# A two-layer recurrent trunk on eight cores: four token groups, two in flight under one schedule, in place of three groups in turn

## The chip, the cores and the metric

One Trainium2 chip, all eight cores; each core runs the same program on its own tokens. The time is that of the slowest core in device microseconds, median of several runs. A program on all eight cores has a second, slower state, in which the cores of one die (0 to 3 or 4 to 7), sometimes both, show a lower granted clock; comparisons here use fast runs alone. PE is TensorE, PEld its weight loads, DVE VectorE, ACT ScalarE, POOL GpSimd, SP SyncE. The granted clock is the share of PE's full clock that the profile shows. PSUM banks are the eight buffers that the matmuls of this program write to.

## The reference, cut to what matters

```python
def trunk(x, ...):                       # layer 0: even mixer (GLA and HGRN2 heads); layer 1: odd mixer (retention)
    for l in range(2):
        nw = norm_w[l]
        x = x + 0.5 * rmsnorm(swiglu(rmsnorm(x, nw[0]), gate[l, 0], up[l, 0], down[l, 0]), nw[1])
        m = mixer(rmsnorm(x, nw[2]), state, ...)      # chunked recurrence, carries a state along the sequence
        x = x + rmsnorm(m, nw[3])
        x = x + 0.5 * rmsnorm(swiglu(rmsnorm(x, nw[4]), gate[l, 1], up[l, 1], down[l, 1]), nw[5])

def swiglu(x, w_gate, w_up, w_down):
    return (silu(x @ w_gate) * (x @ w_up)) @ w_down   # 1024 -> 2816 -> 1024
```

A core has one prompt sequence of 2048 tokens and 16 samples of 8 tokens with states of their own: 2176 tokens, 1024 channels. A group of tokens goes through six stages in order: feed-forward network (FFN), even mixer, FFN, FFN, odd mixer, FFN. Every stage starts with a norm of the residual `x` (pre-norm) and ends with a norm of its own output that is added to `x` (post-norm). So between two stages of one group nothing but norm work can be done. Two groups depend on each other only through the mixers' states.

## The kernel before: the parts concerned

Three groups of 768, 768 and 640 tokens, in turn. Every operation is recorded with its dependences and an estimated cost; a list scheduler then reorders each engine's instructions within a window of 512, and fences (`S.barrier`) stand around the mixers:

```python
for g, tiles in enumerate(GROUP_TILES):                 # 3 groups
    dma_sp(X[:, :, 0:nt], xv[:, :, col0:col0 + nt], ...)
    for l in range(2):
        prenorm(l, 0, nt); ffn(l, 0, nt); postnorm_residual(l, 1, nt, True)
        prenorm(l, 2, nt)
        S.barrier()
        mixer_even(g, tiles, nt) if l == 0 else mixer_odd(g, tiles, nt)
        S.barrier()
        out_proj(...); postnorm_residual(l, 3, nt, False)
        prenorm(l, 4, nt); ffn(l, 1, nt); postnorm_residual(l, 5, nt, True, ...)
# PSUM banks are named for a purpose
PSA, PSB, PSC, PSN = PS[0:2], PS[2:4], PS[4:6], PS[6]
```

The FFN's gate, the statistics of a norm (squares, a matmul with a matrix of ones, logarithm and exponential) and a mask in the mixer, which goes head by head:

```python
act(SGT[..], pg, AF.Silu, ...)                          # one ScalarE function, with a table of its own
tt(HB[:, jj, ..], SGT[..], pu, ALU.mult, ...)
...
for kc in range(nch): act(XN[:, kc, ..], src(kc), AF.Square, ...)     # rms_stats
for kc in range(nch): mm(PSN, ONES, XN[:, kc, ..], ...)
act(LNT, PSN, AF.Ln, ...); act(RS, LNT, AF.Exp, ..., scale=-0.5)
...
for h in range(4):
    tt(PT[..][:, h*128+64:h*128+128], psc[:, h*128+64:h*128+128], MASK0[..], ALU.mult, ...)
```

## Time and profile before

| | before |
|---|---|
| median of the first 4 runs | 4512.52 us (4509.89 to 4714.66) |
| matmuls / DVE / ACT instructions | 21,738 / 3656 / 3002 |
| PE busy, mean granted clock of the profiled core | 75%, 0.84 |
| DMA share of the two data queues | 39.7% + 8.1% |

The prediction below shows the slices and the stages. Two more views of the profile before are used later. First the busy line and the chain that ended last (shares of the span by engine); PE is 61% of that chain, so nearly 40% of the time the end hung on something else:

```profile
PE 3395.3 (75%) x21738; PEld 2074.6 (46%) x21738; DVE 1727.7 (38%) x3656; ACT 1470.8 (33%) x3002; POOL 336.1 (7%) x640
...
PE 61%; DVE 17%; DMA 7%; issue 7%; ACT 6%; SPq 1%; DVEq 1%; ACTq 0%; POOLq 0%
```

Then PE's waits (who waited, for whom, total us, times, longest). `XN` holds the squares and the normalised input: 341.8 us are waits of the statistics for ScalarE's squares, at the borders of stages. Three of them (43.8, 44.6 and 42.2 us) stand at the start and at the two changes of group, where the squares themselves waited for the load of the tokens. `S0B` is one of the mixers' own tiles:

```profile
PE PS L528 <- ACT XN L541: 341.8, 232, 44.6
PE PS L528 <- ACT S0B L541: 130.5, 48, 8.0
...
```

### The profile page before, as it was taken

The page shows a single profiled execution, that of the slowest core. Times are in us where ns is not written, and L with a number is a line of the kernel's source. Part 1 is how long each engine was busy: PE and PEld are TensorE (multiplying, and loading weights), DVE is VectorE, ACT ScalarE, POOL GpSimd, SP SyncE. Part 2 cuts the span into 40 slices and gives each one's busy share as a digit, 9 for nine tenths or more (in the row PEclk, how much of TensorE's full clock was granted, in tenths as well). Part 3 has the DMA queues.
Part 4 walks back from the last instruction along what each step waited for, and adds up shares of the span by engine and source line. Part 5 has one row for each costly group of instructions (what it writes and reads, how often), then busy time and mean ns, then how long its engine had stood idle before and what let it go on. Part 6 is the DMA issues. An engine that isn't in the chain of part 4 may idle for free.

```text
span 4504.0 us, 65698 instructions; the slowest of 8 cores (4488.4 to 4504.0 us)
## 1 busy us (share of the span) xinstructions
PE 3395.3 (75%) x21738; PEld 2074.6 (46%) x21738; DVE 1727.7 (38%) x3656; ACT 1470.8 (33%) x3002; POOL 336.1 (7%) x640
## 2 busy tenths in 40 slices
PE   5956698978796977489888779596536987664487
PEld 3633364645453544345445546373224665431255
DVE  2144514157423143531335641314453234455433
ACT  1235322234421223532224432224343223332232
POOL 1100010100010000001000001010000110000010
PEclk9977799989798987689999879797657998875598
DMA  6622264634355542246453336473224755676554
GB/s 121 94 40 44 46 101 75 102 61 76 60 87 111 92 67 43 41 71 104 75 90 72 77 56 103 103 116 53 61 68 99 121 93 87 148 207 194 172 90 84
DMA packets 172824, 405.79 MB, mean 90 GB/s; under 512 B 18112, under 2 KB 46672, under 8 KB 172496
## 3 DMA queue, kind: packets, MB, share of 16 engines
q0 software_dynamic: 91472, 286.47, 39.7%
q1 hardware_dynamic: 81024, 115.11, 8.1%
q8 instruction: 185, 3.03, 0.3%
q14 instruction: 143, 1.17, 0.1%
HBM read 632.51 MB, written 55.44 MB: 153 GB/s over the span
## 4 chain that ended last, share of the span: by engine, by line
PE 61%; DVE 17%; DMA 7%; issue 7%; ACT 6%; SPq 1%; DVEq 1%; ACTq 0%; POOLq 0%
PE PS L528 60%; DVE TMP L557 5%; ACT YB L541 3%; DVE X L545 3%; DMA ret_s<-S0F 2%; DVE YB L545 2%; DMA S0F<-sret 2%; DMA X<-xT 2%; DVE S0F L557 1%; DVE PT L545 1%; DVE XN L557 1%; ACT L541 1%; SPq L521 1%; DVEq L296 1%; ACT XN L541 1%
## 5 line engine op out<-in xcount | busy, mean ns | idle before, releaser
L528 PE MATMUL PS<-XN,WS 128*128 128x384 bf16 (+1 forms) x10992 | 1820.8, 327 | 172.3 <-ACT YB L541 59.2
L528 PEld LDWEIGHTS PS<-XN,WS 128*128 128x128 bf16 x10992 | 1090.9, 100 | 861.6 <-issue 290.9
L528 PE MATMUL PS<-HB,WD 128*128 128x384 bf16 (+1 forms) x5376 | 845.5, 320 | 24.8 <-DVE HB L545 24.8
L545 DVE TENSOR_TENSOR HB<-SGT,PS 128x384 bf16<-128x384 f32 (+1 forms) x528 | 280.7, 532 | 1296.5 <-PE PS L528 1292.4
L528 PEld LDWEIGHTS PS<-HB,WD 128*128 128x128 bf16 x5376 | 529.8, 99 | 336.1 <-issue 41.4
L541 ACT ACTIVATE SGT<-PS 128x384 f32<-128x384 f32 (+1 forms) x528 | 250.0, 473 | 993.4 <-PE PS L528 989.9
L528 PE MATMUL PS<-XN,ONES 128*128 128x384 bf16 (+1 forms) x576 | 175.4, 387 | 382.7 <-ACT XN L541 341.8
L541 ACT ACTIVATE YB<-PS 128x384 f32<-128x384 f32 (+2 forms) x432 | 204.0, 472 | 457.7 <-PE PS L528 430.2
L528 PEld LDWEIGHTS PS<-XN,ONES 128*128 128x128 bf16 x576 | 57.8, 103 | 493.4 <-issue 479.3
L525 POOL DMA_DIRECT2D WS<-wgu x264 | 139.4, 528 | 1682.4 <-PE PS L528 1634.6
L541 ACT ACTIVATE XN<-YB 128x384 bf16<-128x384 f32 (+1 forms) x288 | 145.5, 505 | 257.9 <-DVE YB L545 236.2
L528 PE MATMUL PS<-WS,XN 128*128 128x256 bf16 x1632 | 210.5, 283 | 24.3 <-DMA WS<-ewin 22.6
L541 ACT ACTIVATE XN<-X 128x384 bf16<-128x384 f32 (+1 forms) x288 | 140.4, 502 | 259.4 <-DVE X L545 160.8
L545 DVE TENSOR_TENSOR YB<-PS,YB 128x384 f32<-128x384 f32 (+1 forms) x204 | 109.2, 535 | 239.8 <-PE PS L528 239.8
L528 PEld LDWEIGHTS PS<-WS,XN 128*128 128x128 bf16 x1632 | 162.5, 102 | 57.2 <-issue 30.5
L557 DVE SCALAR_TENSOR_TENSOR XN<-X,NW,RS 128x384 bf16<-128x384 f32 (+1 forms) x288 | 147.5, 588 | 81.9 <-PE PS L528 49.6
L541 ACT ACTIVATE S0B<-S0F 128x1024 bf16<-128x1024 f32 (+2 forms) x96 | 83.6, 877 | 266.5 <-DMA S0F<-sret 181.4
L528 PE MATMUL PS<-VX,KDT 128*128 128x512 bf16 (+2 forms) x224 | 87.5, 451 | 98.6 <-DVE S0F L557 89.7
L557 DVE SCALAR_TENSOR_TENSOR S0F<-S0F,PS 128x512 f32<-128x512 f32 x128 | 87.8, 686 | 181.3 <-ACT S0B L541 122.2
L528 PE MATMUL PS<-YB 128*128 128x64 bf16 (+2 forms) x408 | 70.3, 240 | 99.2 <-ACT YB L541 36.3
L525 POOL DMA_DIRECT2D WD<-wd x192 | 101.4, 529 | 565.8 <-PE PS L528 549.0
L557 DVE SCALAR_TENSOR_TENSOR TMP<-YB,NW,RS 128x384 f32<-128x384 f32 (+1 forms) x96 | 57.1, 595 | 220.7 <-PE PS L528 211.9
(105 smaller groups left out, 2511.1 us busy)
## 6 DMA issues: line engine op xcount, KB each, us to landing
WS<-wgu POOLq DMA_DIRECT2D x264, 512.0 KB, 6.0
WD<-wd POOLq DMA_DIRECT2D x192, 352.0 KB, 5.0
WS<-owin POOLq DMA_DIRECT2D x72, 512.0 KB, 6.3
S0F<-sret SPq DMA_DIRECT2D x64, 512.0 KB, 4.7
ret_s<-S0F SPq DMA_DIRECT2D x128, 256.0 KB, 3.9
WS<-ewin POOLq DMA_DIRECT2D x30, 512.0 KB, 5.5
WD<-owout POOLq DMA_DIRECT2D x24, 512.0 KB, 6.2
X<-xT SPq DMA_DIRECT2D x2, 3072.0 KB, 29.7
```

Source lines behind the costliest of these rows:

```text
L296: eng.wait_ge(self.esem[src], val)
L521: return S.dma("sp", lambda e, o=out, i=in_: e.dma_start(out=o, in_=i), key, reads, writes, nbytes=nb)
L525: return S.dma("pool", lambda e, o=out, i=in_: e.dma_start(out=o, in_=i), key, reads, writes, nbytes=nb)
L528: return S.op("pe", lambda e, o=out, l=lhsT, r=rhs, a=start, b=stop: e.matmul(o, l, r, start=a, stop=b), reads, writes, cost=max(fsz(rhs), ...
L541: return S.op("act", lambda e, o=out, i=in_, f=func, k=kw: e.activation(out=o, in_=i, func=f, **k), reads, writes, cost=fsz(out) / 1400.0 ...
L545: return S.op(eng, lambda e, o=out, a=in0, b=in1, p=op: e.tensor_tensor(out=o, in0=a, in1=b, op=p), reads, writes, cost=fsz(out) / 960.0 + ...
L557: return S.op("dve", lambda e, o=out, a=in0, x=sc, b=in1, p=op0, q=op1: e.scalar_tensor_tensor(out=o, in0=a, scalar=x, in1=b, op0=p, op1=q ...
```

## The change

The intent is to keep PE busy through mixers and norms with the FFN of another group. The diff rewrites most of the program (1227 added lines, 1125 removed); its core, with cuts:

```diff
-GROUP_TILES = [[0, 1, 2, 3, 4, 5], [6, 7, 8, 9, 10, 11], [12, 13, 14, 15, 16]]
-NTM = 768
-WINDOW = 512
+NG = 4                                  # groups of 544 tokens: 512 of the prompt and 4 samples
+BN = [256, 288]                         # column blocks of one group
...
+class Sched:                            # one list scheduler over all engines and the whole program
+    CAP = {"F": 6, "M": 5}              # PSUM banks that the FFN chain and the mixer chain may hold, of 8
+    MFRAC = 0.85
...
-for g, tiles in enumerate(GROUP_TILES): ...            # FFN, fence, mixer, fence, FFN
+    F(0, 0, 0)                          # F(slot, group, which): stages of one slot run side by side
+    for pr in range(2):
+        a, b = 2 * pr, 2 * pr + 1
+        ...
+        M(sl, a, 0); F(sl, b, 0); sl += 1
+        F(sl, a, 1); M(sl, b, 0); F(sl, a, 2); sl += 1
+        F(sl, b, 1); M(sl, a, 1); F(sl, b, 2); sl += 1
+        F(sl, a, 3); M(sl, b, 1); ...
...
-act(SGT[bi % 2][:, 0:bn], pg[:, 0:bn], AF.Silu, ...)
+act(e, PV(pg[b], 0, BN[b]), AF.Exp, [], re_, scale=-1.0)
+act(e, e, AF.Ln, re_, re_, bias=1.0)
+act(e, e, AF.Exp, re_, re_, scale=-1.0)
+tt(e, PV(pg[b], 0, BN[b]), e, ALU.mult, re_, re_)
...
-for h in range(4):
-    tt(PT[pk][:, h * 128 + 64:h * 128 + 128], psc[...], MASK0[:, kind, 64:128], ALU.mult, ...)
+tt(pv[:, :, 64:128], PV(psc, ...), MASK[:, 64:128].unsqueeze(1).to_broadcast([128, 4, 64]), ALU.mult, ...)
...
+    pend.append((m, b))                 # statistics of a block's post-norm run while the next block is projected
+    if len(pend) > 2: stats_mm(pns[b_], b_, m_, Yv(s, m_, b_), RY(s, m_, b_))
```

A PSUM tile gets whichever bank is free when the scheduler places it. Weights are read four times instead of three.

## The prediction

> **What bounds the kernel now.** I read the cores' spans first: 4488 to 4504 us at a granted clock of 0.841 to 0.846, both dies alike, so a fast run (one of the four timed runs, 4714.66 us, is slow; I predict the fast state). Then the 40 slices of the page:
>
> ```profile
> ## 2 busy tenths in 40 slices
> PE   5956698978796977489888779596536987664487
> ...
> PEclk9977799989798987689999879797657998875598
> DMA  6622264634355542246453336473224755676554
> ```
>
> PE swings between 9 and 4, the clock swings with it, and no other engine is full where PE is not. So this is not one bound but stages in turn. The table of windows, cut at stage borders that I found from the long matmul runs of the timeline, tells them apart (columns: stretch, length, busy us of PE, PEld, DVE, ACT and POOL with instruction counts, granted clock, DMA share, GB/s):
>
> ```profile
> 0.00:53.00 53.00, 6.00 (x17) 2.18 (x18) 4.20 (x14) 9.11 (x20) 6.14 (x15) 1.00 0.78 156
> ...
> 227.00:533.00 306.00, 178.39 (x1025) 103.15 (x1024) 150.00 (x357) 142.60 (x318) 14.68 (x28) 0.72 0.25 40
> 533.00:707.00 174.00, 173.62 (x1059) 103.68 (x1057) 39.85 (x73) 39.60 (x78) 19.53 (x37) 0.99 0.59 97
> 707.00:734.00 27.00, 9.60 (x32) 2.98 (x31) 20.24 (x35) 12.89 (x24) 0.53 (x1) 0.68 0.13 23
> ...
> 908.00:1250.00 342.00, 258.14 (x1730) 156.53 (x1729) 199.84 (x412) 146.26 (x272) 17.42 (x33) 0.85 0.34 62
> ...
> 3453.00:3597.00 144.00, 143.48 (x1052) 103.03 (x1051) 32.01 (x67) 34.91 (x77) 19.86 (x38) 1.00 0.73 117
> ...
> 3768.00:4325.00 557.00, 312.29 (x2186) 179.33 (x2184) 267.09 (x546) 190.97 (x316) 17.26 (x33) 0.68 0.58 157
> ...
> 4471.00:4504.00 33.00, 3.06 (x19) 1.62 (x16) 17.00 (x33) 3.83 (x7) 0.00 (x0) 0.56 0.21 80
> ```
>
> 533:707 is one feed-forward (FFN) of 768 tokens: PE full, DVE and ACT under a quarter. 227:533 is the even mixer with its norms, 908:1250 the odd mixer, 3768:4325 the odd mixer of the last group with all sample states: PE 56 to 75% and part of that at a low clock, DVE and ACT about half, each waiting for another. 707:734 is norm work between two FFNs. There are twelve FFN stretches, 8 of 174 us and 4 of 144 (640 tokens): 1968 us. The other 2536 us hold little PE work. How little needs the price of a matmul:
>
> ```profile
> 140.33 57.36 PE L528 MATMUL PS<-XN,WS 128*128 128x384 bf16 x352
> ...
> 311.70 7.15 PE L528 MATMUL PS<-WS,XN 128*128 128x256 bf16 x64
> ```
>
> 57.36/352 = 163 ns for 384 columns. 7.15 us for 64, less about 0.2 us for the last one's drain, is 109 ns for 256. Both fit columns/2.4 + 2 ns. In a dense stretch 128-column matmuls start about 55 ns apart, which I take as the least price. Over all 21,738 matmuls of this kernel (6.98 million columns) that is 2992 us at full clock. So PE has 2992 us to do in 4504, and 1512 us are idle or lost to the low clock.
>
> **What the Trainium skill says.** "Perfetto Trace Analysis", section Optimization Strategy: where the contended engine changes over time, interleave those regimes. That is this change. "TensorE: Matmul & The Clock Gate", Part 1: PE is at 4/8 clock after an idle window and at 8/8 after some 3.4 us of work; the trace agrees (0.72 in the mixer, 0.99 to 1.00 in the FFNs). The same part says that three cores of a die at dense matmuls bring a current limit of 13/16. The fast run does not show it: eight cores dense together, clock 1.00 on each. The slow run may be it; no trace of one is here. Same page, Back-to-back issue gap: N/2.4 + 2.5 ns, as measured above. "ScalarE: Activation LUTs", What ACT_TABLE_LOAD costs: 1283 ns each; the trace has 55 of 1283 ns, 70.6 us in all.
>
> **The change part by part.** Counts are from the two instruction orders.
>
> 1. Schedule. Three groups of 768, 768, 640 tokens, one after another with fences around mixers, become four of 544 with two in flight: the FFN of one beside the mixer of the other. A global list scheduler orders every engine and hands eight PSUM banks to both chains. Only the first and the last of 16 FFNs stand alone. Cutting the PE order into pieces of 50 us of work, each piece from about 130 to about 2950 has both chains, mixer share 5 to 32 us. So the idle 1512 us is what is attacked.
>
> 2. PE work. 27,864 matmuls of 7.07 million columns, mostly 256 and 288. By the price above: FFN chain 2008 us, mixers 1042, sum 3050; that is 58 us more than before (6126 more matmuls at 2 ns and 0.09 million columns, mostly partial sample tiles). Weight loads take 98 ns each (103.68/1057) and hide behind 109.
>
> 3. ACT. Silu becomes exp, ln, exp on ACT and a multiply on DVE, so that all functions share a table; 50-odd loads (about 70 us) go, 1408 FFN activations and the gates' come. Prices from rows of the trace: 384 ns for 256 columns out of PSUM, 417 out of SBUF, 0.83 ns a further column. Sum: 2094 us (1159 in FFNs, 935 in mixers) against 1471. Each triple is dependent, and dependent ones in the trace leave gaps of 0.05 to 0.1 us, so some 2250 us of hold.
>
> 4. DVE. Price 421 ns for 256 columns, 554 for 384; with a per-partition scalar 476 and 610. Sum about 2290 us (1095 and 1190) against 1728. Four prompt tiles' small products are fused, the silu multiply and the evacuation of every down projection come new.
>
> 5. DMA. Weights are read four times instead of three: 764 MB instead of 573. The cast queue took 39.7% of 4504 = 1788 us for 286.5 MB landed; 382 MB at that rate is 2383 us, and at the rate of the 640-token FFNs (117 GB/s at share 0.73 to 0.75, so 158) 2420. The other queue's 8.1%, 365 us, stays. Sum near 2780 us of 16 full engines. An FFN alone would need 34.6 MB in 126 us, 137 GB/s landed, share about 0.87.
>
> Floors, then: PE 3050, DMA 2780, DVE 2290, ACT 2250. PE still binds. On top of it: start about 30 us (53 now; a 256-token block of 1 MB starts the work in place of 3 MB); tail about 22 (33 now; 32 DVE pieces of half a us, then a short store); four places where an FFN follows the FFN of the same group, and two where the X buffer must be stored and reloaded, 25 to 45 us of norm or transfer each, half covered by the other chain: about 100. Then the small waits of a fixed order at 62 to 82% load on three other units: here I choose 6% of 3050, about 190; the odd mixer, which already overlaps two heads, loses 25%, but it has nothing else to run. 3050 + 30 + 22 + 100 + 190 is about 3390; I say 3400.
>
> **The rivals.**
> A. The bound moves to ACT/DVE latency: a gate tile holds its bank through three activations and a multiply, about 1.7 us plus queueing, and only six banks serve the FFN chain. For it: 1.5 us of ACT per tile against 1.85 us of PE per pair of tiles in the gate phase, plus the mixer's own ACT work. Against: sums are 25% under PE's. If true, PE is near 80% busy: 3700 to 3800.
> B. DMA becomes the bound: 2780 us is 91% of PE's floor, the rings are four deep, and pool issues stand in one order for three rings. For it: share already 0.75 in the 640-token FFNs. Against: FFN and mixer traffic mix, and mixers ask less per us. If true, 3450 to 3600, with PE waits on WF, WD or WM.
> C. Clock limit: 90% dense PE beside busy ACT, DVE and DMA may draw more current than any stage of the kernel before. At 13/16, 3050 becomes 3754, and the total about 3850 to 3950. Against: 1.00 in 174 us of density. I give it one in eight.
> D. The scheduler's costs are so close that waits nearly vanish: 3200 to 3250.
>
> **Range and chances.** D sets the low end, 3220; A or part of C the high, 3720. Even C is 13% under 4512, so slower needs an order that stalls everywhere. Faster 0.96, same 0.02, slower 0.02.
>
> **What would show it.** Point 1: no slice of PE under 8 but the first and the last, clock about 0.97 or higher over the span (a mean near 0.8 in dense slices is C). Point 2: matmul count 27,864 and, per dense window, 109 to 122 ns a matmul. Point 3: one or two table loads; ACT about 2100 us busy. Point 4: DVE about 2300. Point 5: DMA share near 0.8, and PE waits on weight tiles under 50 us in sum (more is B). The chain should be three quarters or more PE; if ACT on Z or DVE on Z and HB leads the waits of PE, A holds. The prediction is wrong if PE idles over 15% of the span, whichever cause.

## The result, and the profile after

| | before | after |
|---|---|---|
| median, all runs of the comparison | 4516.31 us (15 runs, 4504.48 to 4885.66) | 3548.77 us (10 runs, 3544.92 to 3823.44) |
| ratio of fast runs | 1 | 0.7854 [0.7829, 0.7878] |
| PE busy / granted clock | 75% / 0.84 | 92% / 0.96 |
| DVE / ACT busy us | 1728 / 1471 | 2024 / 1864 |

Ratios here are the mean time of one kernel's fast runs over that of the other's fast runs of the same rounds, so not quite the ratio of the medians. A ratio times 4516 us gives the differences below: the change took off 0.2146 of 4516, 969 us. The fast runs of the kernel before averaged 4505 to 4520 us from one set of rounds to another, so such a difference can be off by some 15 us; where it matters, the mean of the fast runs themselves stands beside it (3549.7 us for the changed kernel).

The page of the changed kernel: busy us, the slices (each digit tenths of a 40th of the span), the two data queues with their share of 16 engines, and the chain that ended last.

```profile
PE 3259.0 (92%) x27777; PEld 2588.9 (73%) x27864; DVE 2023.7 (57%) x4866; ACT 1864.4 (53%) x4744; POOL 444.5 (13%) x845
...
PE   5989999998998989979999898999989899899987
...
PEclk9999999999999989989999899999999999999989
DMA  8967778786896957888867785887768789588865
...
q0 software_dynamic: 118096, 382.10, 67.2%
q1 hardware_dynamic: 61344, 117.27, 9.9%
...
PE 74%; DMA 13%; DVE 6%; issue 4%; ACT 2%; SPq 0%; DVEq 0%; ACTq 0%; POOL 0%; POOLq 0%
```

The swings of PE are gone, and the clock with them. The small dips that are left have a common look. In the table of windows (stretch, length, busy us of PE, PEld, DVE, ACT and POOL with counts, granted clock, DMA share, GB/s) a steady stretch stands beside the start, three borders and the tail:

```profile
0.00:40.00 40.00, 5.92 (x17) 1.78 (x17) 5.80 (x20) 9.68 (x24) 13.56 (x29) 1.00 0.95 214
...
190.00:200.00 10.00, 6.01 (x23) 2.58 (x22) 10.00 (x26) 3.48 (x9) 0.00 (x0) 0.50 0.01 2
...
230.00:400.00 170.00, 162.58 (x1457) 132.30 (x1461) 102.80 (x250) 106.25 (x269) 20.07 (x38) 1.00 0.78 134
...
440.00:450.00 10.00, 4.32 (x16) 1.88 (x15) 10.00 (x26) 5.89 (x16) 0.00 (x0) 0.56 0.00 0
...
3390.00:3400.00 10.00, 0.40 (x1) 0.10 (x1) 10.00 (x27) 0.00 (x0) 0.00 (x0) 0.50 0.40 164
...
3528.00:3546.50 18.50, 1.26 (x10) 0.66 (x7) 12.87 (x33) 1.99 (x5) 0.00 (x0) 0.65 0.30 121
```

In the steady stretch PE does 1457 matmuls in 162.58 us, 112 ns each, at full clock. At 190, 440 and 3390 us DVE is busy all ten of ten, the DMA queues stand still at the first two (nobody frees a weight tile), and PE does little, at half clock. What DVE does there shows in the timeline of its instructions from 189 to 200 us (start, length, instruction, count):

```profile
189.20 0.83 DVE L487 TENSOR_TENSOR X<-X,Z 128x288 f32<-128x288 f32 x2
189.93 0.95 DVE L498 SCALAR_TENSOR_TENSOR Z<-Z,NWH,RSF 128x288 f32<-128x288 f32 x2
...
193.12 6.69 DVE L498 SCALAR_TENSOR_TENSOR Z<-X,NW,TS 128x256 bf16<-128x256 f32 x16
199.72 0.79 DVE L487 TENSOR_TENSOR Z<-PS,Z 128x256 f32<-128x256 f32 x2
```

and PE beside it:

```profile
193.64 0.77 PE L519 MATMUL PS<-SQM,ONES 128*128 128x288 bf16 x2 [0.83 <-ACT SQM L483]
196.64 3.68 PE L519 MATMUL PS<-Z,WM 128*16 128x256 bf16 x16 [2.23 <-DVE Z L498]
```

The post-norm of an FFN (scaling and residual addition, alternating, since 181 us) and then the normalisation of the mixer's input hold DVE until 199.7 us. PE has only statistics matmuls, a few at a time, behind ScalarE's squares, and from 196.6 us the first projection of the mixer: sixteen matmuls of 256 columns in 3.68 us, 230 ns each, at half clock. The gate multiply of the other group's FFN (the line at 199.72) stands behind the norm in DVE's order. So two things meet: one group has nothing but norm work, and the other's gate comes after it. Whether PE could go on sooner if that multiply came first is not shown; PE's own order, fixed beforehand too, has the mixer's projection next.

I counted what such places cost by cutting the span into pieces of 10 us and taking, in each, its length less PE's busy time times the granted clock as lost. The sum is 367 us: 34 in the first 40 us, 18 in the tail, 234 in 49 pieces that lose more than 2 us (143 of these in pieces where DVE is at least 90% busy; they lie around some fourteen places), and 81 in all other pieces. Of the 234, 163 us are idle and 71 are PE at work at a low clock. The trace of this core lacks 87 of the 27,864 matmuls, which count as lost (some 10 us, an estimate at 112 ns each); the mean of the eight cores is 351 us in sum, 33, 16, 236 and 66. The remaining 3179 us hold the work that I had priced at 3050; the 129 us above that I take for drains and gaps inside what counts as busy.

PE's waits, against those of before: the longest sum is 46 us.

```profile
PE PS L519 <- ACT SQP L483: 46.0, 67, 12.2
...
PE PS L519 <- DVE NOML L493: 31.2, 1, 31.2
PE PS L519 <- DVE Z L498: 31.1, 14, 10.5
...
PE PS L519 <- DMA WD<-wd: 19.1, 27, 1.9
```

### The profile page after: what moved, and what is told of

Same layout as the page of the kernel before. It is cut to its first block, busy times and chain, and to the rows that moved or that the text cites. A ratio compares the mean times of both kernels' runs of the same rounds, so it can differ in the third digit from the quotient of the medians.

```text
span 3546.5 us, 84038 instructions; the slowest of 8 cores (3516.9 to 3546.5 us)
## 1 busy us (share of the span) xinstructions
PE 3259.0 (92%) x27777; PEld 2588.9 (73%) x27864; DVE 2023.7 (57%) x4866; ACT 1864.4 (53%) x4744; POOL 444.5 (13%) x845
## 4 chain that ended last, share of the span: by engine, by line
PE 74%; DMA 13%; DVE 6%; issue 4%; ACT 2%; SPq 0%; DVEq 0%; ACTq 0%; POOL 0%; POOLq 0%
PE PS L519 74%; DMA WD<-wd 4%; DVE Z L498 3%; DMA S0F<-sret 3%; DMA ret_s<-S0F 2%; DMA WM<-ewin 1%; DVE X L487 1%; ACT Z L483 1%; DMA WM<-owout 1%; DMA S0F<-sgla 1%; DVE Z L487 1%; DMA EG<-c_eg 1%; ACT SQP L483 0%; DMA hgrn_s<-S0F 0%; PE PS L532 0%
## 5 line engine op out<-in xcount | busy, mean ns | idle before, releaser
L519 PE MATMUL PS<-Z,WF 128*128 128x256 bf16 (+1 forms) x11264 | 1457.0, 282 | 48.2 <-DVE Z L498 20.4
L519 PEld LDWEIGHTS PS<-Z,WF 128*128 128x128 bf16 x11264 | 1092.4, 99 | 286.8 <-issue 76.8
L519 PE MATMUL PS<-HB,WD 128*128 128x256 bf16 (+1 forms) x5632 | 710.4, 280 | 23.2 <-DMA WD<-wd 19.1
L483 ACT ACTIVATE Z<-Z 128x288 f32<-128x288 f32 (+1 forms) x1408 | 596.4, 427 | 92.7 <-ACT Z L483 0.8
L487 DVE TENSOR_TENSOR Z<-PS,Z 128x256 f32<-128x256 f32 (+1 forms) x704 | 306.7, 437 | 416.6 <-ACT Z L483 413.7
L483 ACT ACTIVATE Z<-PS 128x256 f32<-128x256 f32 (+1 forms) x704 | 274.6, 391 | 459.9 <-PE PS L519 455.7
L519 PE MATMUL PS<-Z,WM 128*128 128x288 bf16 (+3 forms) x3392 | 476.9, 288 | 22.6 <-DVE Z L498 8.9
L487 DVE TENSOR_TENSOR HB<-PS,Z 128x256 bf16<-128x256 f32 (+1 forms) x704 | 305.8, 437 | 196.5 <-PE PS L519 155.2
L519 PEld LDWEIGHTS PS<-Z,WM 128*128 128x128 bf16 (+1 forms) x3392 | 333.9, 100 | 107.7 <-issue 35.5
L519 PE MATMUL PS<-WM,Z 128*128 128x256 bf16 (+1 forms) x1920 | 250.0, 279 | 14.7 <-DMA WM<-ewin 13.9
```

Source lines behind the costliest of these rows:

```text
L483: return S.op("act", lambda e: e.activation(out=A(out), in_=A(in_), func=func, **kw), reads, writes, cost=fsz(out) / 1200.0 + 0.18, ps=psl ...
L487: return S.op(eng, lambda e: e.tensor_tensor(out=A(out), in0=A(in0), in1=A(in1), op=op), reads, writes, cost=fsz(out) / 960.0 + 0.16, ps=p ...
L519: ins = e.matmul(A(o), l, r, start=a, stop=b, skip_group_check=True)
```

## The experiments

Two questions. Where does the gain come from: from the overlap of two groups, as the prediction had it, or from the other parts? And what are the some 150 us by which the kernel came in above the prediction: VectorE's norm work, ScalarE, weights, the start, or the chain of dependences at the borders as such? Twelve kernels; each was timed in three rounds, `start` in five. The record's verdict by the 2% rule is "unclear" for `serial`, `add8`, `halfdma` and `oneact`, in whose rounds only three of the seven runs of the kernel before were fast; their intervals rest on these three.

### serial: the overlap alone undone

One stage at a time in every engine's order, group after group, all else as in the changed kernel (right values). Weight transfers may still run ahead.

```diff
+if o.dma is None and o.stage.idx > cur: continue      # the scheduler takes only operations of the current stage
-    CAP = {"F": 6, "M": 5}
+    CAP = {"F": 8, "M": 8}
-    F(0, 0, 0) ... F(sl, b, 3)
+    for g in range(NG):
+        for k, (c, f) in enumerate([(F, 0), (M, 0), (F, 1), (F, 2), (M, 1), (F, 3)]): c(6 * g + k, g, f)
```

> The changed kernel with only the overlap undone: in every engine's order all work of one FFN or mixer stands before that of the next, group after group; the fused instructions, the four groups, the free use of eight PSUM banks and the activations stay. Theory 1 (the prediction's): the overlap of FFN and mixer is nearly the whole gain, so the time goes back to 4300 us or more. Theory 2: the other parts of the change (fused small instructions, no fences around mixers, banks shared freely) give half of the gain or more, so the time is 3800 to 4050 us, with PE near 80% busy and about 600 us or less of the gain left to the overlap.

Measured: 3994.81 us median, ratio 0.8861 [0.8841, 0.8881]. So the overlap is worth 0.1007 of 4516, 455 us (442 by the means of the fast runs), and the rest of the change 0.1139, 514 us. That is the overlap taken out of the full change; adding it alone to the kernel before was not tried, and the parts may help each other. The serial kernel's windows, an even mixer, an odd one and an FFN of 544 tokens:

```profile
1158.00:1324.00 166.00, 120.59 (x943) 85.40 (x946) 120.97 (x295) 100.35 (x245) 10.58 (x20) 0.85 0.47 92
1599.00:1875.00 276.00, 213.49 (x1709) 152.11 (x1720) 167.09 (x393) 122.80 (x304) 19.59 (x37) 0.84 0.62 139
1324.00:1452.00 128.00, 125.68 (x1069) 104.93 (x1068) 48.65 (x111) 59.95 (x148) 19.52 (x37) 0.99 0.80 130
```

Summed over all groups, against the stages of the kernel before: even mixers 679 for 1013 us, odd mixers 1078 for 1240, FFNs 2062 for 1968, the norms between FFNs and groups together with start and tail some 110 us less. For the even mixer the kernel before has PE idle 306 less 178 us for 768 tokens, 0.17 us a token; here it is 166 less 121 for 544, 0.08. ACT's work for a token is the same (143 us for 768 tokens, 100 for 544) and DVE's some 14% more (150 and 121). So the mixers got faster on their own, by waiting less and not by working less.

### oneact and halfdma: rivals A and B of the prediction

`oneact` leaves out two of the three activations of the gate, `halfdma` moves half the bytes of each weight tile (after each ring's first tiles); both give wrong values and keep the rest.

```diff
 act(e, PV(pg[b], 0, BN[b]), AF.Exp, [], re_, scale=-1.0)
-act(e, e, AF.Ln, re_, re_, bias=1.0)
-act(e, e, AF.Exp, re_, re_, scale=-1.0)
 tt(e, PV(pg[b], 0, BN[b]), e, ALU.mult, re_, re_)
```

> Of the three activations of each FFN gate tile only the first stays, with the multiply (wrong result on purpose): 1408 activations of 427 ns, 596 us of ACT, go. Theory 1 (ACT does not set the pace, the gate tiles' latency is covered by the free banks): within 1.5% of 3549. Theory 2 (rival A of the prediction, banks held through the activations): 5% or more faster, under 3380 us.

```diff
+    h = int(out.shape[1]) // 2
+    out, in_ = out[:, 0:h], in_[:, 0:h]          # half of the weight tile
```

> After the first loads of each buffer every weight load moves half of its bytes, with the instruction order unchanged (wrong result on purpose). Theory 1 (DMA is hidden; PE's waits on weight tiles sum to 36 us in the trace): at most 1.5% faster, 3500 us or more. Theory 2 (rival B of the prediction; the chain that ended last gives DMA 13%): 3450 us or less, 3% or more faster.

Measured: `oneact` 3579.53 us in the median of fast and slow runs, 3558.2 in the mean of its three fast ones, ratio 0.7905 [0.781, 0.8001], a wide interval round the changed kernel's 0.7854, with ACT busy 1353.5 in place of 1864.4 us. There is no gain, so ScalarE's load and the time that a gate tile holds its bank do not set the time. `halfdma` 3480.21 us, ratio 0.7723 [0.7706, 0.7741]: 59 us less (70 by the means of the fast runs). Between the two theories: weights cost something, about 2%, far from a bound. In the mean of the eight cores the loss outside the borders falls from 66 to 46 us and that in the pieces over 2 us from 236 to 206 (counted as above), so weights take part at the borders too.

### add8, post8, norm8: the width of the norm work at the borders

Each makes a further part of the norms narrower (8 columns in place of 256 or 288; wrong values). `post8` and `norm8` are planned with the full costs, so that PE's order stays that of the changed kernel; `add8` was planned with its own smaller costs, and its order differs. In `norm8` the rest of each tile of squares is filled with ones at the start.

```diff
-tt(X[s][b][:, kc, :], X[s][b][:, kc, :], y, ALU.add, ...)                          # add8: the additions
+tt(X[s][b][:, kc, 0:8], X[s][b][:, kc, 0:8], y[:, 0:8], ALU.add, ...)
-stt(y, y, wt[:, c:c + 1], rs, ALU.mult, ALU.mult, ...)                              # post8: also the scaling
+stt(y[:, 0:8], y[:, 0:8], wt[:, c:c + 1], rs[:, 0:8], ALU.mult, ALU.mult, ...)
-act(sq[:, 0:bn], src, AF.Square, rsrc, [rsq])                                       # norm8: also all squares
+act(sq[:, 0:8], src[:, 0:8], AF.Square, rsrc, [rsq])
```

> The residual adds of the norms work on 8 columns of each block instead of all 256 or 288 (wrong result on purpose; the dependences stay). That takes about 0.27 us from each of 384 DVE instructions, 104 us of DVE in all, most of it at the 14 stage borders where DVE is full, PE half idle and its clock low. Theory 1 (the norms on DVE set the length of each border): 3440 to 3500 us, 1.5 to 3% faster. Theory 2 (the borders are the latency of the norm chain or of the fixed order, or PE's lost time lies elsewhere): within 1% of 3549.

> The changed kernel with the scaling and the residual addition of every post-norm on 8 columns in place of 256 or 288 (wrong values on purpose), about 207 us of VectorE work removed; the orders of TensorE and ScalarE are the same as in the changed kernel. If VectorE's norm work sets how long the fourteen stage borders cost, most of what they lose (some 200 us) comes back: 3400 to 3450 us, and the pieces of the span in which VectorE is full and TensorE is half idle are gone. If the borders are set by the latency of the chain (squares, statistics, Ln and Exp, scaling, all in a fixed order) rather than by VectorE's throughput, less than what the additions alone gave comes on top: 3480 us or more. If nothing at the borders matters, 3500 us as without the additions.

> The kernel with post-norm scaling and additions on 8 columns, and now also the squares of all norms on 8 columns (wrong values on purpose; the rest of each tile is filled with ones once). TensorE's order is the same. If ScalarE's squares and VectorE's additions by their width are what the borders wait for, the remaining loss at the borders (195 us in pieces that lose over 2 us) falls by half or more: 3400 us or less. If the borders are a matter of the chain's number of links and of an order fixed beforehand, with little for TensorE to do in it from the other group: 3470 to 3490 us.

| | median us | ratio | less than after, us | DVE busy | ACT busy | lost in pieces over 2 us | of it DVE 90% busy |
|---|---|---|---|---|---|---|---|
| after | 3548.77 | 0.7854 | | 2023.7 | 1864.4 | 234 | 143 |
| add8 | 3501.28 | 0.7769 [0.7751, 0.7787] | 38 | 1937.9 | 1865.9 | 202 | 58 |
| post8 | 3493.02 | 0.7735 [0.7691, 0.7779] | 54 | 1838.6 | 1861.2 | 195 | 27 |
| norm8 | 3479.22 | 0.7693 [0.7663, 0.7724] | 73 | 1841.1 | 1710.2 | 182 | 25 |

By the means of the fast runs the three are 50, 58 and 73 us below the changed kernel; the mean of the eight cores for the loss in pieces over 2 us is 236, 192, 187 and 172. `add8` itself decided nothing: 3501 us is at the edge of its first theory's range.

With the additions and the scaling narrow, DVE is no longer full at the borders, and the same ten microseconds of `post8` read:

```profile
190.00:200.00 10.00, 7.74 (x32) 3.82 (x33) 6.70 (x17) 3.68 (x9) 0.37 (x1) 0.51 0.00 0
...
440.00:450.00 10.00, 9.47 (x68) 6.34 (x66) 6.35 (x17) 6.26 (x16) 1.59 (x3) 0.89 0.31 46
```

The border at 440 is nearly mended, the one at 190 is not: DVE is busy 6.7 of the ten us, and PE still runs at half clock with 32 matmuls. Over the span the loss at the borders falls only from 234 to 195, and to 182 with the squares narrow too. My theory that the width of the post-norm's work on VectorE sets the borders would have had `post8` at 3400 to 3450, so it falls. The numbers fit the rival, the chain of dependences: most of the loss, some 180 us, is there with hardly any width left in post-norm and squares. What no run narrowed is the pre-norm's scaling: at this border of `post8` it takes 6.8 us of VectorE from 187.4 to 195.0 us, and PE's projection waits for it. A narrow instruction still takes its fixed time, and there are as many of them in a row:

```profile
L487 DVE TENSOR_TENSOR X<-X,Z 128x8 f32<-128x8 f32 x320 | 48.7, 167 | 1.0 <-DVE Z L498 0.6 <-DVE X L487 0.3
L498 DVE SCALAR_TENSOR_TENSOR Z<-Z,NWH,RSF 128x8 f32<-128x8 f32 x256 | 46.2, 221 | 19.4 <-ACT RSF L483 19.2 <-issue 0.2
```

(In these lines: busy us, mean ns of one, then idle time before them and what ended it.) Of `norm8`'s 182 us, 55 are PE at work at a low clock and 127 are idle. How the idle time divides between the length of this chain, the pre-norm's width and an order that was fixed with other costs in mind is left open; for that the plan itself would have to change.

### merge4 and pool2: two ways to relieve VectorE with right values

```diff
-tt(X[s][b][:, kc, :], X[s][b][:, kc, :], y, ALU.add, ...)             # one addition for each of 8 channel blocks
+if kc % MG == MG - 1:                                                 # merge4: MG = 4, on VectorE
+    tt(xf, xf, zy, ALU.add, rx + ry, rx, eng=RES)                     # pool2: MG = 2, on GpSimd
```

> The changed kernel with the residual additions of a post-norm merged, one instruction for four channel blocks (right values). That leaves out three of four instructions' fixed costs, some 20 to 30 us of VectorE work, all of it at the borders. Border bound by VectorE: 3520 to 3535 us. If the later release of the first block costs as much as the merging saves: 3549 us, the same.

> The changed kernel with the residual additions on GpSimd, two channel blocks to an instruction (right values). That takes some 104 us from VectorE at the borders, and the kernel without the additions took 3501 us. If GpSimd adds quickly enough and its queue of weight transfers is not held up: 3500 us or a little less. Rival: GpSimd also issues the weight transfers in order, the additions wait there for the norms and hold up the transfers behind them, and GpSimd's addition is slower than VectorE's: 3560 to 3700 us, with waits for weight tiles that are not there now.

`merge4`: 3546.24 us, ratio 0.7852 [0.7806, 0.7898]: the same. The additions take 124 us in place of 152, and nothing comes of it. That the first block is now released only with the fourth would explain it, but no run shows that.

`pool2`: 3653.73 us, ratio 0.8095 [0.8059, 0.8131]: 109 us more. The expected waits for weight tiles did not come; PE's waits for weights sum to 25 us, for 36 in the changed kernel, and the longest sum is 58.3 us for the squares. What happened shows in two groups of instructions, GpSimd's addition and VectorE's scaling beside it:

```profile
L489 POOL TENSOR_TENSOR X<-X,Z 128x576 f32<-128x576 f32 x80 | 117.7, 1472 | 35.7 <-DVE Z L500 33.8 <-ACT SQP L485 1.0 <-ACT SQM L485 0.6
...
L500 DVE SCALAR_TENSOR_TENSOR Z<-Z,NWH,RSF 128x288 f32<-128x288 f32 x128 | 125.4, 1046 | 0.0
```

The same scaling in the changed kernel:

```profile
L498 DVE SCALAR_TENSOR_TENSOR Z<-Z,NWH,RSF 128x288 f32<-128x288 f32 x128 | 60.3, 513 | 0.0
```

GpSimd adds 576 columns in 1472 ns, and VectorE's instruction with two inputs, which alternates with these additions, takes twice its time; the pre-norm's scaling, the same kind of instruction mostly at other times, stays at 511 ns for 513. The same run shows it side by side: of its pre-norm scalings of 256 columns (`Z<-X,NW,RSP`) the 16 that coincide with a GpSimd addition take 1010 ns, the 112 others 476. VectorE ends with 2080.8 us busy, more than the 2023.7 with the additions on it. The move gives back more than it takes off. The plan had priced a 576-column addition on GpSimd at 0.76 us (the cost formula of the kernel), so the order was fixed with a wrong cost as well; how the 109 us divide between the two is not separated.

### silu and b_nosilu: the table switches

`silu` undoes the gate's part of the change; `b_nosilu` takes the Silu, and with it the switches, out of the kernel before (wrong values).

```diff
-act(e, PV(pg[b], 0, BN[b]), AF.Exp, [], re_, scale=-1.0)              # silu, against the changed kernel
-act(e, e, AF.Ln, re_, re_, bias=1.0)
-act(e, e, AF.Exp, re_, re_, scale=-1.0)
-tt(e, PV(pg[b], 0, BN[b]), e, ALU.mult, re_, re_)
+act(e, PV(pg[b], 0, BN[b]), AF.Silu, [], re_)
-act(SGT[bi % 2][:, 0:bn], pg[:, 0:bn], AF.Silu, ...)                  # b_nosilu, against the kernel before
+act(SGT[bi % 2][:, 0:bn], pg[:, 0:bn], AF.Exp, ...)
```

> The changed kernel with the gate made as before, by one activation of ScalarE's own Silu in place of exponential, logarithm, exponential and a multiply. Saves some 500 us of ScalarE work and some of VectorE's, but ScalarE's order then goes between the Silu table and the exponential table some 420 times, at 1.283 us each about 540 us. If table loads on the way from a bank to its release cost time: 3600 to 3800 us. If ScalarE's load does not matter at all (two of three activations left out gained nothing): within 1% of 3549 us. If the loads stop the overlap of mixer and FFN: over 3900 us, towards what one stage at a time took.

> The kernel before with its Silu replaced by an exponential (wrong values on purpose), so that its 55 loads of ScalarE's tables are gone; nothing else is changed. They take 70.6 us, and 96 us of idle time lie before them. If they lie on the path: 70 to 140 us less than before, 4370 to 4440 us. If TensorE was busy meanwhile: 4510 us, the same.

`silu`: 3735.36 us, ratio 0.8271 [0.821, 0.8332]: 188 us more, in the range of the first theory. Its loads, and the first of PE's waits, on the gate's tile, which was 0.6 us in the changed kernel:

```profile
L483 ACT ACT_TABLE_LOAD x421 | 540.1, 1283 | 128.6 <-PE PS L519 116.0 <-DMA X<-x 6.4
```

```profile
PE PS L519 <- ACT Z L483: 71.7, 58, 3.8
```

`b_nosilu`: 4465.53 us, ratio 0.9885 [0.9852, 0.9919]: 52 us less than before, between the two theories; the interval lies clear of 1. So the 70.6 us of loads in the kernel before lay mostly on the path, but the gain of that part, by itself, is small. With two chains interleaved, in the order that the scheduler makes, the same Silu needs 421 switches and costs 188 us; the two further activations cost nothing (`oneact`). So this overlap needs the longer gate, more than that gains by itself. The scheduler of the changed kernel does not know of tables; an order that gathers the Silus was not tried.

### unfuse: the mixer's operations over four heads, one by one

```diff
-tt(pv[:, :, 64:128], PV(psc, ...), MASK[...].to_broadcast([128, 4, 64]), ALU.mult, ...)
+for h in range(4): tt(pv[:, h:h+1, 64:128], ..., ALU.mult, ...)        # so for masks, decays and head norms
```

> The changed kernel with its small mixer operations over four heads (masks, decays, norms of heads) undone into one VectorE operation for each head, as in the kernel before (right values). If those fused operations carry a good part of what the mixers gained: 3620 to 3750 us. If VectorE has room for them beside the other group's FFN: 3550 to 3590 us.

Measured: ratio of the fast runs 0.8018 [0.7978, 0.8059], 74 us more (two fast runs, 3619.59 and 3628.0 us; the median of 3841.99 is that of slow runs). DVE has 5950 instructions in place of 4866 and, on a core of the undisturbed die, 2135.6 us busy. Right values. A part of the gain, between the two theories' ranges.

The profiled run of this kernel was a slow one, which shows what that state is: die 0 has a median of 3824.7 us at a clock of 0.875, die 1 of 3615.6 at 0.957. Cores 0, 2 and 5 of the same run, a dense stretch of each (window 250 to 350 us):

```profile
250.00:350.00 100.00, 96.29 (x714) 71.90 (x713) 53.35 (x183) 58.06 (x146) 9.88 (x19) 0.81 0.68 116
```

```profile
250.00:350.00 100.00, 93.00 (x808) 74.01 (x809) 71.70 (x238) 72.19 (x187) 12.13 (x23) 1.00 0.71 127
```

```profile
250.00:350.00 100.00, 94.46 (x812) 74.92 (x810) 71.28 (x236) 72.36 (x188) 11.60 (x22) 0.98 0.70 127
```

So it is not the whole of die 0 at once. Cores 0 and 1 are at 0.80 to 0.81 here, cores 2 and 3 at 1.00 and 0.98; in the window 2150 to 2200 us it is the other way round, 1.00 on cores 0 and 1 and 0.81 on cores 2 and 3.

### start: the constants that the first norm waits for

```diff
+R_ONE, R_NW = R(), R()                              # own dependences for the ones and the norm weights, loaded first
-mms([(..., ONES[:, :], sq[:, 0:bn], ...)], [rsq, R_C])
+mms([(..., ONES[:, :], sq[:, 0:bn], ...)], [rsq, R_ONE])
```

> The changed kernel with the matrix of ones and the norm weights given a dependence of their own, so that the first norm no longer waits for all the constants (right values, otherwise the same program). TensorE's one wait for the vector made last from the constants was 31 us. If it lay on the path that sets the end: 10 to 20 us less, 3530 to 3540 us. If the first weights or the tokens arrive no sooner than that: 3549 us, the same.

Measured: 3549.64 us, ratio 0.7849 [0.7825, 0.7873]: the same. Right values. The 31 us wait is gone; a shorter one takes its place:

```profile
PE PS L519 <- DMA ONES<-c_ones: 13.4, 1, 13.4
```

and the windows show PE ahead early and slowed right after, with the DMA share at 0.93 or more all the while (0.92 in the changed kernel's second window):

```profile
0.00:40.00 40.00, 18.98 (x85) 9.20 (x86) 12.13 (x36) 19.46 (x51) 13.57 (x29) 1.00 0.96 213
40.00:140.00 100.00, 89.92 (x755) 74.61 (x753) 43.44 (x101) 52.05 (x130) 14.29 (x27) 0.95 0.93 142
```

```profile
40.00:140.00 100.00, 97.55 (x796) 79.36 (x796) 49.88 (x115) 61.38 (x156) 13.22 (x25) 0.98 0.92 136
```

PE does 13 us more in the first 40 us and 8 less in the next 100. Of what was left, the borders took most: in the mean of the eight cores the loss at the start falls from 33 to 21 us and that in pieces over 2 us rises from 236 to 244. The start was worth nothing on its own, and no version with right values beat the changed kernel.

## Why the prediction was right, and where it was not

**Time.** Predicted 3400, range 3220 to 3720, faster with 0.96; measured 3548.77, a ratio of 0.7854. The direction and the range held. The sum is 149 us short.

**The sum, term by term.** Predicted 3050 + 30 + 22 + 100 + 190; by the count of lost time above, 3050, 34, 18, 234, and 81 + 129 = 210. So the start, the tail and the small waits came out within 20 us; for the small waits that is luck, since their 6% was chosen and not worked out. The mis-sized term is "four places where an FFN follows the FFN of the same group, and two where the X buffer must be stored and reloaded, ... about 100": the profile has some fourteen such places, not six, and they lose 234 us. I had counted only borders at which one chain has no other stage to go to, and had taken the remaining borders of FFN and mixer as covered by the other chain. The trace shows that they are not: the other chain's gate multiply stands behind the norm in VectorE's one order, and PE has little but statistics, at half clock. `norm8` shows that narrower norm work takes back only 73 us of the time; which link sets the rest is open.

One reading was loose too. The 2536 us outside the FFN stretches do not "hold little PE work": PE is busy 3395 us in all and 1961 in the twelve stretches, so 1434 us of it lie there, partly at a low clock. The sum of 2992 does not rest on that sentence.

**Where the gain comes from.** The prediction put the attacked time, "the idle 1512 us", to the schedule of two groups in flight. `serial` shows that undoing the overlap gives back 455 of 969 us; 514 come without any overlap, most of it in the mixers of one group by themselves. Of these 514 the experiments name 52 (table switches, in the kernel before) and 74 (operations over four heads, in the changed one). If these add up, the other nearly 390 us, which banks not named for a purpose, the fences that are gone and statistics within the projections may share, I did not take apart. That the total nevertheless came out is no proof of the attribution: it was a floor plus losses, whichever part removes the idle time.

**The floors.** PE's price held: 112 ns a matmul in the steady stretch, between 109 and 122. DMA predicted 2780 us, measured 77.1% of 3546.5, 2734. ACT predicted 2094 and DVE 2290, measured 1864 and 2024, some 11% under: I multiplied counts by mean durations, and neighbours on one engine overlap in the records (128 scalings of 513 ns make 66 us, and their row says 60.3 busy).

**Rivals.** A (activations hold banks): falls with `oneact`. B (weights): waits for weight tiles sum to 36 us, under the 50 I had set, and halving the bytes gives 59. C (a clock of 13/16): fast runs show 0.96 in the mean and 1.00 in the dense stretch; it is what the slow state shows (0.81 on two cores of one die at a time). D (waits nearly vanish): no.

**Signs.** One slice in the middle is at 7 where I had said none under 8; the clock is 0.962 to 0.967 where I had said 0.97; one table load, and PE 74% of the chain where I had said three quarters; PE idles 8% of the span, under the 15 that would have refuted it.

## What to carry to other kernels

When two chains are interleaved, count the places where one of them has only short dependent work and ask whether the other's release of buffers stands behind that work on the same in-order engine; those places cost here more than twice what was allowed for them. Before a gain is put down to an overlap, run the same program with the overlap alone undone: here it was less than half. An engine that has room can still be the wrong place for work if it slows its neighbour.

## What the Trainium skill lacked or had wrong

- "TensorE: Matmul & The Clock Gate", Part 1 (peak-current limiter): it has 13/16 follow once three cores of a die run dense matmuls. In the fast state all eight cores run dense and the clock is 0.99 to 1.00 (230 to 400 us of the changed kernel); 0.81, which is 13/16, shows only in the slow state. The page has the whole die go to it; in the slow run of `unfuse` it is two cores at a time, 0.80 and 0.81 on cores 0 and 1 beside 1.00 and 0.98 on cores 2 and 3 from 250 to 350 us. That the state differs from execution to execution of one program is not on the page.
- The same page, "Back-to-back issue gap": it gives some 131 ns for 512 columns in a sustained stream with weight loads and calls the N/2.4 + 2.5 formula too high for large N. Here 352 matmuls of 384 columns with their weight loads took 163 ns each, which the formula gives, so 131 for 512 is out of reach.
- "GPSIMD Engine Reference", "1. Specifications": it names the contention with VectorE instructions of two SBUF inputs without a size, and no page measures it for this pair of instructions. Here such an instruction of 288 columns went from 513 to 1046 ns beside GpSimd's additions. Its two-input rate (section 3.1, about 2.6 cycles an element, 2.2 ns by the page's 1.2 GHz as an estimate) agrees: between 1326 ns for 512 columns and 1472 for 576 lie 2.3 ns a column.
- "ScalarE: Activation LUTs", "What ACT_TABLE_LOAD costs": 1283 ns for the load agrees, 421 times. The drain of about 1380 ns for every switch does not show: all idle time before those 421 loads is 128.6 us, 0.3 us each, and after a load the next activation begins 11 ns later in the median.
